# Boundary additions moved to VectorE, transposes per token tile, and narrower first feed-forward pieces in a two-block transformer kernel

## The chip, the cores and the metric

The kernel runs on one NeuronCore of one Trainium2 chip. The metric is the device time of one execution in microseconds (us). Before the change the median of 3 runs is 1402.76 us (1401.82 to 1402.99).

## What is computed

Two transformer blocks run one after the other over 512 tokens of width 1024, in float32. Each block is a mixer (a convolution and attention pair in the first, retention and latent attention in the second), a residual addition, a normalisation, a feed-forward network of hidden width 2816 with a gate and an up half, and a second residual addition. What matters here is the place between two such parts, called a boundary below. Cut to that, the reference says:

```python
x = x + ga1 * rmsnorm(y, post_mix_g)                   # boundary 1, gated
h = rmsnorm(x, pre_ffn_g) * (1.0 + sc2) + sh2
gate, up = jnp.split(h @ w_ffn_in, 2, axis=-1)
x = x + ga2 * rmsnorm(y_ffn, post_ffn_g)               # boundary 2, gated
h = rms_norm(x, attn_norm_w);  proj = h @ w_in_2
x = x + mixed @ w_out                                  # boundary 3, plain
u = rms_norm(x, ffn_norm_w) @ w_up
```

Both norms divide by the root of the mean of squares over the 1024 features of a token.

## The kernel before, in words

The 512 tokens are four token tiles of 128 (tt = 0 to 3), and 1024 features are eight blocks of 128 (kb). Every float32 matrix product is made of three matmuls on split operands (a high part and a low part of each side); `mm3` (lines 201 to 204) issues them, so its three lines carry nearly all the TensorE time.

Weights arrive as slabs of 128x1024. `emit_slab` (lines 175 to 187) loads one into a staging buffer `w_st` (two of them), ScalarE casts it to `w_hi` (line 184), and VectorE, or GpSimd for a few named slabs, subtracts to get `w_lo` (line 207). There are four `w_hi` and four `w_lo` buffers. `slab(key, ahead)` also starts the slabs that follow.

Before each boundary, `gemm_tok` (line 280) makes a product that has tokens on partitions: `wo` before boundary 1, `fout` before boundary 2, `wo2` before boundary 3. The last four slabs stay resident, and the token tiles are finished one after the other, each yielding its PSUM banks, two halves of 512 features. All four `w_hi` buffers are held until the last tile is done.

`boundary` (line 338) takes each token tile as it is yielded. `update` (line 321) adds it to the residual `x`. In the gated case (`grow` given, boundaries 1 and 2) it takes the squares' sums of both halves on ScalarE (`sumsq`, line 247), makes `r` with `rstd` (VectorE line 235, then a power on GpSimd, line 239), multiplies each half on VectorE (line 331) and adds half 0 on VectorE and half 1 on GpSimd (line 334). In the plain case both additions are on VectorE (line 325). Then `norm_of` (line 250) takes one sum of squares over all 1024 features, a second `rstd` (line 233), and writes the normalised tile `xn` (VectorE, line 252).

When `tt` is in `ends`, `to_h` (line 273) transposes the collected `xn` tiles: for each kb, one 128x128 transpose per tile on TensorE (line 228) into a PSUM bank of `psT`, which has two banks, and then `evac_h` (line 254) writes the bank to `hh` and `hl`: ScalarE for `hh` (line 258 or 263), and for `hl` VectorE alone (line 259), or, where there is a bias (boundary 1), VectorE (line 268) and GpSimd (line 207). With `ends=(1, 3)` (boundaries 1 and 3) these are two groups of two tiles, so 256 columns per instruction. With `ends=(1,2,3)` (boundary 2) they are groups of 2, 1 and 1.

After boundaries 1 and 3, `ffn_in` (line 871) starts with four slabs (two pairs of gate and up) and runs them in two column pieces, `t0` = 0 and 256, so that the first half can start before the last tiles are there. In that loop each of the 4 slabs times 8 kb times 3 lines of `mm3` gives 96 matmuls per piece. All later slabs run with 512 columns. After boundary 2 comes a `gemm_tok` on the slabs `c2`, which goes token tile by token tile and has no such pieces.

The order of instructions on each engine is not the program's: the kernel is built in a tile context that schedules over a simulated timeline (line 1448), and the engines' queues then run in that fixed order. `boundary`, `to_h` and `ffn_in` are thus interleaved by the builder.

Of the kernel before, what the change touches and what calls it, by code (L numbers as in the profile page):

```python
# [8 lines left out]
F32 = mybir.dt.float32  # L9
# [4 lines left out]
ALU = mybir.AluOpType  # L14
# [5 lines left out]
KB = 8  # L20
# [75 lines left out]
def build(tc, nc, a):  # L96
    stacks = []

    def pool(name, bufs=1, side="left", **kw):
        s = ExitStack()  # L100
        p = s.enter_context(tc.tile_pool(name=name, bufs=bufs, side=side, reuse_waits="tile", **kw))
        stacks.append(s)
        return p, s

    def close(*ss):
        for s in ss:
            s.close()
# [27 lines left out]
    def pp():  # L135
        Banks.at = (Banks.at + 1) % 6
        if Banks.both and Banks.at % 3 == 0:
            return conv_bank()
        ps_p = psP.tile([128, 512], F32, tag="p", name="ps_p")
        return ps_p  # L140
# [5 lines left out]
    eps1k = const.tile([128, 1], F32)  # L146
# [5 lines left out]
    an32 = const.tile([128, 16], F32)  # L152
# [5 lines left out]
    hh = hpool.tile([128, KB, S], F32R)  # L158
    hl = hpool.tile([128, KB, S], F32R)
# [33 lines left out]
    def slab(key, ahead=2):  # L193
        assert ORDER[W.got] == key, (ORDER[W.got], key)
        W.got += 1
        if W.nxt < W.got:
            emit_slab()
        prefetch(ahead)
        return W.ready.pop(key)

    def mm3(out, lh, ll, rh, rl, start, stop):
        nc.tensor.matmul(out=out, lhsT=lh, rhs=rh, start=start, stop=False)  # L202
        nc.tensor.matmul(out=out, lhsT=lh, rhs=rl, start=False, stop=False)  # L203
        nc.tensor.matmul(out=out, lhsT=ll, rhs=rh, start=False, stop=stop)  # L204
# [11 lines left out]
    def mtile(ps, w, rh, rl, nk, width, c0=0, t0=0, t1=S):  # L216
        wh, wl = w
        for k in range(nk):
            c = k * width + c0
            mm3(  # L220
                ps[:, t0:t1], wh[:, c:c + 128], wl[:, c:c + 128],
                rh[:, k, t0:t1], rl[:, k, t0:t1], k == 0, k == nk - 1,
            )
# [6 lines left out]
    def rstd(ss0, ss1, n_eps):  # L230
        q = sm.tile([128, 1], F32, tag="q", name="q")
        if ss1 is None:
            nc.vector.tensor_tensor(out=q, in0=ss0, in1=n_eps, op=ALU.add)
        else:
            nc.vector.scalar_tensor_tensor(  # L235
                out=q, in0=ss0, scalar=ss1, in1=n_eps, op0=ALU.add, op1=ALU.add
            )
        r = sm.tile([128, 1], F32, tag="r", name="r")
        nc.gpsimd.tensor_tensor(out=r, in0=q, in1=mhalf[:, 0:1], op=ALU.pow)  # L239
        return r  # L240

    def sumsq(src, jp):
        ss = sm.tile([128, 1], F32, tag="ss", name="ss")
        n = src.shape[1]
        w = 256 if n <= 256 else 1024
        junk = jp.tile([128, w], BF16, tag=f"junk{w}", name="junk", bufs=1)
        nc.scalar.activation(out=junk[:, :n], in_=src, func=AF.Square, accum_out=ss)
        return ss

    def norm_of(x_t, jp, xn):  # L250
        r = rstd(sumsq(x_t, jp), None, eps1k)
        nc.vector.tensor_scalar(out=xn, in0=x_t, scalar1=r, scalar2=None, op0=ALU.mult)
# [20 lines left out]
    def to_h(xns, t0, scale, bias, ep):  # L273
        n = len(xns) * 128
        for kb in range(KB):
            ps = pt()
            transposes(ps, [xn[:, kb * 128:(kb + 1) * 128] for xn in xns])
            evac_h(ps[:, :n], kb, t0, n, scale(kb), bias(kb) if bias else None, ep)
# [39 lines left out]
    def h_operand(k):  # L318
        return hh[:, k, :], hl[:, k, :]

    def update(banks, tt, x_in, x_out, grow, bp):
        if grow is None:
            for hf in range(2):
                cs = slice(512 * hf, 512 * hf + 512)
                nc.vector.tensor_tensor(out=x_out[:, cs], in0=banks[tt, hf], in1=x_in[:, cs], op=ALU.add)
            return
        r = rstd(sumsq(banks[tt, 0], bp), sumsq(banks[tt, 1], bp), eps1k)
        for hf in range(2):
            cs = slice(512 * hf, 512 * hf + 512)
            y = bp.tile([128, 512], F32, tag="y", name="y", bufs=2)  # L330
            nc.vector.scalar_tensor_tensor(
                out=y, in0=banks[tt, hf], scalar=r, in1=grow[:, cs], op0=ALU.mult, op1=ALU.mult
            )
            (nc.vector if hf == 0 else nc.gpsimd).tensor_tensor(
                out=x_out[:, cs], in0=x_in[:, cs], in1=y, op=ALU.add
            )

    def boundary(gen, x_in, x_out, grow, scale, bias, bp, after=None, ends=(1, 3)):
        xns = []
        for tt, banks in gen:  # L340
            xi, xo = x_in(tt), x_out(tt)
            update(banks, tt, xi, xo, grow, bp)
            xn = bp.tile([128, D], F32, tag="xn", name="xn", bufs=3)
            norm_of(xo, bp, xn)
            if after:
                after(tt, xo)
            xns.append(xn)
            if tt in ends:
                to_h(xns, 128 * (tt + 1 - len(xns)), scale, bias, bp)
                xns = []  # L350

    class ADA:
        pool, tag, bufs, nacc = ring, "st", NST, 1
# [96 lines left out]
    for _n in ("pre_mix_g", "pre_ffn_g"):  # L450
        _o = VOFF[_n]
        nc.vector.tensor_scalar(
            out=vec[:, _o:_o + 8], in0=vec[:, _o:_o + 8], scalar1=32.0, scalar2=None, op0=ALU.mult
        )
    _o = VOFF["ada_b"]
    for _i in (_o + 8, _o + 32):
        nc.vector.tensor_scalar(
            out=vec[:, _i:_i + 8], in0=vec[:, _i:_i + 8], scalar1=1.0, scalar2=None, op0=ALU.add
# [5 lines left out]
        out=lat[:, 0:2], in0=vec[:, _o:_o + 2], scalar1=float(np.float32(16.0 * 96.0 ** -0.5)), scalar2=None,  # L464
        op0=ALU.mult,
    )
    nc.vector.tensor_scalar(
        out=lat[:, 2:3], in0=vec[:, _o + 2:_o + 3], scalar1=float(np.float32(np.sqrt(128.0))), scalar2=None,
        op0=ALU.mult,
# [135 lines left out]
    gen = gemm_tok([("v", i) for i in range(4)], h_operand, 512, 2, seg=2)  # L605
# [229 lines left out]
    for p in range(4):  # L835
# [26 lines left out]
    bp, bp_s = pool("bp1")  # L862
    gen = gemm_tok([("wo", k) for k in range(8)], lambda k: (mh[:, k, :], ml_[:, k, :]), D, 4)
    x1t = lambda tt: x1[:, tt, :]
    boundary(
        gen, x1t, x1t, grow1, lambda kb: modA[:, 1, kb:kb + 1], lambda kb: modB[:, 1, kb:kb + 1], bp
    )
# [3 lines left out]
    def ffn_in(tag, evac, extra=None, split=None):  # L871
        first = []
        for m in range(2):
            first.append((pp(), slab((tag, m)), pp(), slab((tag, NF + m), 2 - m)))
        for t0 in (0, 256):
            for g, wg, u, wu in first:
                mtile(g, wg, hh, hl, KB, 128, 0, t0, t0 + 256)
                mtile(u, wu, hh, hl, KB, 128, 0, t0, t0 + 256)
        for m, (g, _, u, _) in enumerate(first):
            evac(m, g, u)  # L880
        for m in range(2, NF):
            if extra:
                extra(m)
            if m >= NF - 4:
                split(m - NF + 4)
            g = pp()
            mtile(g, slab((tag, m)), hh, hl, KB, 128)
            u = pp()
            mtile(u, slab((tag, NF + m)), hh, hl, KB, 128)
            evac(m, g, u)  # L890
# [17 lines left out]
    grow2 = gpool.tile([128, D], F32)  # L908
# [47 lines left out]
    def fin_extra(m):  # L956
        if m in (4, 8, 12, 16):
            ga_row(1, grow2, ad2, m // 4 - 1)
        if m == 4:
            rotary()  # L960

    ffn_in("fin", evac1, fin_extra, g1)
    close(ad2_s, f_s)
    bp, bp_s = pool("bp2")
    gen = gemm_tok([("fout", k) for k in range(NF)], g1, D, 4)
    x2d = nc.dram_tensor("x2_spill", [S, D], F32, kind="Internal").ap()

    def spill(tt, xo):
        nc.gpsimd.dma_start(out=x2d[tt * 128:(tt + 1) * 128, :], in_=xo)

    boundary(gen, x1t, x1t, grow2, lambda kb: an32[:, kb:kb + 1], None, bp, after=spill, ends=(1,2,3))
    close(bp_s, g_s, x_s)


# [41 lines left out]
    for tt, banks in gemm_tok([("c2", i) for i in range(4)], h_operand, 416, 4, seg=2):  # L1016
        b = banks[tt, 0]
        for j, (c0, c1) in enumerate(((0, 256), (256, 384))):
            r = rstd(sumsq(b[:, c0:c1], cp), None, epsq[:, j:j + 1])
# [6 lines left out]
    def win2_group(gi):  # L1026
        return gemm_tok([("win2", 4 * gi + i) for i in range(4)], h_operand, 512, 2, seg=2)
# [10 lines left out]
    for kb in range(3):  # L1038
# [5 lines left out]
            out=cTl[:, kb, :], in0=ps, scalar=sc, in1=cTh[:, kb, :].bitcast(F32), op0=ALU.mult, op1=ALU.subtract  # L1044
# [14 lines left out]
    gen = win2_group(2)  # L1059
# [234 lines left out]
    bp, bp_s = pool("bp3")  # L1294
    gen = gemm_tok([("wo2", k) for k in WO2], lambda i: h_operand(WO2[i]), D, 4)
    boundary(gen, x3t, x3t, None, lambda kb: an32[:, 8 + kb:9 + kb], None, bp)
    close(bp_s)

# [29 lines left out]
    bp, bp_s = pool("bp4")  # L1328
    gen = gemm_tok([("down", k) for k in range(NF)], g2, D, 4)
    for tt, banks in gen:  # L1330
        x_t = x3[:, tt, :]
        ot = bp.tile([128, D], F32, tag="ot", name="ot", bufs=2)
        ss = []
        for hf in range(2):
            cs = slice(512 * hf, 512 * hf + 512)
# [3 lines left out]
        r = rstd(ss[0], ss[1], eps1k)  # L1339
        for hf in range(2):  # L1340
            cs = slice(512 * hf, 512 * hf + 512)
# [110 lines left out]
```

## Time and profile before

| | |
|---|---|
| median of 3 runs | 1402.76 us |
| the profiled execution | 1402.35 us, of which the span of the trace is 1400.6 us |
| TensorE (PE) busy | 1348.2 us, 96% of the span |
| VectorE (DVE), ScalarE (ACT), GpSimd (POOL) busy | 55%, 41%, 24% |
| granted TensorE clock, mean | 0.99 of full speed |

In the profile a line such as L202 is a line of the kernel. PE is the matmul row of TensorE, PEld its weight loads, which overlap with matmuls. A matmul's duration in the trace holds its pipeline, so a stream is read by the distance between starts. A releaser after an arrow is what ended an engine's wait. The times of the boundaries in the trace are about 372 to 424 us (first), 749 to 795 us (second) and 1017 to 1054 us (third).

### The profile page before, as it was taken

How to read it: one execution, taken by the hardware profiler on the slowest of the kernel's cores; microseconds unless marked ns; L12 is line 12 of the kernel's file. 1: busy time of each engine (PE TensorE's matmuls, PEld its weight loads, DVE VectorE, ACT ScalarE, POOL GpSimd, SP SyncE). 2: the span in 40 equal slices, each digit the busy share in tenths (PEclk: the TensorE clock that was granted, in tenths of full speed). 3: DMA queues.
4: the chain of work that ended last, by engine and by line, in shares of the span. 5: the costliest groups of instructions: out<-in, count | busy, mean ns of one | idle time of the engine just before them, and what ended most of it. 6: DMA issues, size and time to landing. Idle time of an engine off the chain costs nothing.

```text
span 1400.6 us, 17393 instructions
## 1 busy us (share of the span) xinstructions
PE 1348.2 (96%) x6686; PEld 1119.8 (80%) x6686; DVE 769.5 (55%) x1203; ACT 581.2 (41%) x953; POOL 334.7 (24%) x337
## 2 busy tenths in 40 slices
PE   6998999999979999999999999999999999999997
PEld 4786787888878888888887788887888888888886
DVE  3399968477356434323334665788257555554334
ACT  4357655332244322222323526777246433333323
POOL 2279855411150000000002534567020000000000
PEclk9998999999989999999999999999999999999999
DMA  8422133566224334433322322011323332323231
GB/s 323 154 76 88 35 120 120 166 200 197 99 68 141 126 125 128 135 91 94 102 91 93 121 91 92 30 33 46 111 86 120 99 98 93 103 91 105 91 97 69
DMA packets 44578, 152.18 MB, mean 109 GB/s; under 512 B 4912, under 2 KB 7344, under 8 KB 44496
## 3 DMA queue, kind: packets, MB, share of 16 engines
q1 hardware_dynamic: 43008, 146.03, 32.4%
q0 software_dynamic: 1344, 4.84, 0.9%
q8 instruction: 52, 0.85, 0.2%
q14 instruction: 30, 0.25, 0.1%
q10 hardware_dynamic: 144, 0.21, 0.0%
HBM read 146.86 MB, written 4.19 MB: 108 GB/s over the span
## 4 chain that ended last, share of the span: by engine, by line
PE 84%; DVE 7%; ACT 3%; issue 2%; POOL 2%; DMA 1%; SPq 0%; POOLq 0%; ACTq 0%; DVEq 0%
PE ps_p L202 17%; PE ps_p L204 16%; PE ps_p L203 16%; PE ps_c L203 8%; PE ps_c L204 8%; PE ps_c L202 7%; PE ps_t L202 2%; PE ps_t L204 2%; PE ps_t L203 2%; PE ps_t L228 2%; DVE kp L719 1%; PE ps_t L679 1%; DVE ps_c L523 1%; PE ps_t L385 1%; DVE w_lo L207 1%
## 5 line engine op out<-in xcount | busy, mean ns | idle before, releaser
L184 ACT CAST w_hi<-w_st 128x1024 fp32r<-128x1024 f32 (+2 forms) x217 | 225.1, 1040 | 386.1 <-PE ps_p L203 138.7
L207 DVE TENSOR_TENSOR w_lo<-w_st,w_hi 128x1024 fp32r<-128x1024 f32 (+2 forms) x179 | 222.4, 1244 | 235.5 <-ACT w_hi L184 233.8
L203 PE MATMUL ps_p<-hl,w_hi 128*128 128x512 f32 (+1 forms) x740 | 279.6, 379 | 0.4 <-POOL hl L207 0.4
L204 PE MATMUL ps_p<-hh,w_lo 128*128 128x512 f32 (+1 forms) x740 | 278.0, 377 | 1.4 <-DVE w_lo L207 1.4
L202 PE MATMUL ps_p<-hh,w_hi 128*128 128x512 f32 (+1 forms) x740 | 276.5, 382 | 1.9 <-ACT hh L263 1.2
L239 POOL TENSOR_TENSOR r<-q,mhalf 128x1 f32<-128x1 f32 x36 | 20.9, 583 | 764.5 <-DVE q L235 716.7
L202 PEld LDWEIGHTS ps_p<-hh,w_hi 128*128 128x128 f32 x740 | 139.2, 191 | 29.9 <-ACT hh L263 2.5
L204 PEld LDWEIGHTS ps_p<-hh,w_lo 128*128 128x128 f32 x740 | 140.9, 190 | 27.4 <-DVE w_lo L207 2.5
L203 PEld LDWEIGHTS ps_p<-hl,w_hi 128*128 128x128 f32 x740 | 141.1, 191 | 25.8 <-POOL hl L207 1.6
L202 PE MATMUL ps_c<-hh,w_hi 128*128 128x512 f32 (+1 forms) x354 | 130.0, 367 | 3.9 <-ACT hh L263 3.1
L203 PE MATMUL ps_c<-hl,w_hi 128*128 128x512 f32 (+1 forms) x354 | 130.8, 370 | 0.4 <-POOL hl L207 0.4
L204 PE MATMUL ps_c<-hh,w_lo 128*128 128x512 f32 (+1 forms) x354 | 128.8, 364 | 0.0
L207 POOL TENSOR_TENSOR w_lo<-w_st,w_hi 128x1024 fp32r<-128x1024 f32 (+1 forms) x38 | 93.8, 2474 | 57.2 <-ACT w_hi L184 49.0
L207 DVE TENSOR_TENSOR gl<-gf,gh 128x512 fp32r<-128x512 f32 x44 | 30.4, 690 | 105.6 <-ACT gh L899 105.6
L899 ACT CAST gh<-gf 128x512 fp32r<-128x512 f32 x44 | 27.4, 622 | 133.4 <-PE ps_p L203 124.1
L202 PEld LDWEIGHTS ps_c<-hh,w_hi 128*128 128x128 f32 x354 | 67.6, 191 | 15.3 <-ACT hh L263 3.3
L203 PEld LDWEIGHTS ps_c<-hl,w_hi 128*128 128x128 f32 x354 | 67.2, 190 | 10.9 <-POOL hl L207 0.6
L204 PEld LDWEIGHTS ps_c<-hh,w_lo 128*128 128x128 f32 x354 | 67.5, 191 | 10.2
L204 PE MATMUL ps_p<-w_hi,gl 128*128 128x512 f32 x176 | 68.6, 390 | 0.0
L203 PE MATMUL ps_p<-w_lo,gh 128*128 128x512 f32 x176 | 68.5, 389 | 0.0
L202 PE MATMUL ps_p<-w_hi,gh 128*128 128x512 f32 x176 | 68.5, 389 | 0.0
L523 DVE SCALAR_TENSOR_TENSOR ps_c<-upad,vec,ps_c 128x512 f32<-128x512 f32 x87 | 60.6, 747 | 0.7
(428 smaller groups left out, 2564.3 us busy)
## 6 DMA issues: line engine op xcount, KB each, us to landing
ad<-in_ada SPq DMA_DIRECT2D x48, 512.0 KB, 4.1
w_st<-in_w_fin SPq DMA_DIRECT2D x44, 512.0 KB, 3.7
w_st<-in_w_up SPq DMA_DIRECT2D x44, 512.0 KB, 3.4
w_st<-in_w_win SPq DMA_DIRECT2D x22, 512.0 KB, 3.6
w_st<-in_w_fout SPq DMA_DIRECT2D x22, 512.0 KB, 3.5
w_st<-in_w_down SPq DMA_DIRECT2D x22, 512.0 KB, 3.5
w_st<-in_w_gate SPq DMA_DIRECT2D x16, 512.0 KB, 3.7
w_st<-in_w_wo SPq DMA_DIRECT2D x16, 512.0 KB, 3.8
```

Source lines behind the costliest of these rows:

```text
L184: nc.scalar.copy(w_hi[:, :n], w_st[:, :n])
L202: nc.tensor.matmul(out=out, lhsT=lh, rhs=rh, start=start, stop=False)
L203: nc.tensor.matmul(out=out, lhsT=lh, rhs=rl, start=False, stop=False)
L204: nc.tensor.matmul(out=out, lhsT=ll, rhs=rh, start=False, stop=stop)
L207: (eng or nc.vector).tensor_tensor(out=out, in0=src, in1=hi.bitcast(F32), op=ALU.subtract)
L228: nc.tensor.transpose(out=ps[:r, j * 128:(j + 1) * 128], in_=s, identity=ident)
L239: nc.gpsimd.tensor_tensor(out=r, in0=q, in1=mhalf[:, 0:1], op=ALU.pow)
L385: nc.tensor.matmul(out=ps[32 * b:32 * b + 32, 0:256], lhsT=cact[:, 4 * hf + b, :], rhs=ad[:, b, :], start=hf == 0, stop=hf == 1,)
L523: nc.vector.scalar_tensor_tensor(out=out, in0=src, scalar=w, in1=acc, op0=ALU.mult, op1=ALU.add)
L679: nc.tensor.matmul(out=ps[:, kb * 128:S], lhsT=vt(kb, h), rhs=a_slice(at[j], kb, 0, n), start=first, stop=kb == NT - 1 and j == 0,)
L719: nc.vector.tensor_tensor_scan(out=kp[:, :n][:, ::-1], data0=kp[:, :n][:, ::-1], data1=zero.broadcast_to([128, n]), initial=1.0, op0=ALU.m ...
L899: nc.scalar.copy(gh, gf[:, k, :])
```

## The change

The addition of half 1 in the gated case moves from GpSimd to VectorE. The sum of squares of the new `x` is taken per half, right after each half's addition, instead of once over 1024 features, and `rstd` adds the two. The default `ends` goes from (1, 3) to (0, 1, 3), and boundary 2 from (1, 2, 3) to (0, 1, 2, 3). `ffn_in` runs its first four slabs in pieces of 128, 128 and 256 columns in place of 256 and 256.

```diff
     def update(banks, tt, x_in, x_out, grow, bp):
-        if grow is None:
-            for hf in range(2):
-                cs = slice(512 * hf, 512 * hf + 512)
-                nc.vector.tensor_tensor(out=x_out[:, cs], in0=banks[tt, hf], in1=x_in[:, cs], op=ALU.add)
-            return
-        r = rstd(sumsq(banks[tt, 0], bp), sumsq(banks[tt, 1], bp), eps1k)
+
+        if grow is not None:
+            r = rstd(sumsq(banks[tt, 0], bp), sumsq(banks[tt, 1], bp), eps1k)
+        ss = []
         for hf in range(2):
             cs = slice(512 * hf, 512 * hf + 512)
-            y = bp.tile([128, 512], F32, tag="y", name="y", bufs=2)
-            nc.vector.scalar_tensor_tensor(
-                out=y, in0=banks[tt, hf], scalar=r, in1=grow[:, cs], op0=ALU.mult, op1=ALU.mult
-            )
-            (nc.vector if hf == 0 else nc.gpsimd).tensor_tensor(
-                out=x_out[:, cs], in0=x_in[:, cs], in1=y, op=ALU.add
-            )
-
-    def boundary(gen, x_in, x_out, grow, scale, bias, bp, after=None, ends=(1, 3)):
+            y = banks[tt, hf]
+            if grow is not None:
+                y = bp.tile([128, 512], F32, tag="y", name="y", bufs=2)
+                nc.vector.scalar_tensor_tensor(
+                    out=y, in0=banks[tt, hf], scalar=r, in1=grow[:, cs], op0=ALU.mult, op1=ALU.mult
+                )
+            nc.vector.tensor_tensor(out=x_out[:, cs], in0=y, in1=x_in[:, cs], op=ALU.add)
+            ss.append(sumsq(x_out[:, cs], bp))
+        return ss
+
+    def boundary(gen, x_in, x_out, grow, scale, bias, bp, after=None, ends=(0, 1, 3)):
         xns = []
         for tt, banks in gen:
             xi, xo = x_in(tt), x_out(tt)
-            update(banks, tt, xi, xo, grow, bp)
+            ss = update(banks, tt, xi, xo, grow, bp)
             xn = bp.tile([128, D], F32, tag="xn", name="xn", bufs=3)
-            norm_of(xo, bp, xn)
+            nc.vector.tensor_scalar(out=xn, in0=xo, scalar1=rstd(ss[0], ss[1], eps1k), scalar2=None, op0=ALU.mult)
...
-        for t0 in (0, 256):
+        for t0, t1 in ((0, 128), (128, 256), (256, 512)):
             for g, wg, u, wu in first:
-                mtile(g, wg, hh, hl, KB, 128, 0, t0, t0 + 256)
-                mtile(u, wu, hh, hl, KB, 128, 0, t0, t0 + 256)
+                mtile(g, wg, hh, hl, KB, 128, 0, t0, t1)
+                mtile(u, wu, hh, hl, KB, 128, 0, t0, t1)
...
-    boundary(gen, x1t, x1t, grow2, lambda kb: an32[:, kb:kb + 1], None, bp, after=spill, ends=(1,2,3))
+    boundary(gen, x1t, x1t, grow2, lambda kb: an32[:, kb:kb + 1], None, bp, after=spill, ends=(0, 1, 2, 3))
```

## Rows read from the trace of the kernel before

**Rows 1.** The page's first part: engine, busy us, share of the span, instructions.

```profile
PE 1348.2 (96%) x6686; PEld 1119.8 (80%) x6686; DVE 769.5 (55%) x1203; ACT 581.2 (41%) x953; POOL 334.7 (24%) x337
```

**Rows 2.** Stretches of the three boundaries: length, busy us by engine, clock, DMA share, GB/s.

```profile
core 0: us, PE busy (x) PEld busy (x) DVE busy (x) ACT busy (x) POOL busy (x), PEclk, DMA share, GB/s
...
386.00:393.00 7.00, 0.64 (x3) 0.41 (x4) 4.76 (x8) 3.88 (x9) 2.36 (x3) 0.79 0.58 188
393.00:400.30 7.30, 6.75 (x29) 5.94 (x30) 6.63 (x10) 4.46 (x10) 4.17 (x5) 0.50 0.48 144
400.30:405.00 4.70, 4.31 (x38) 4.07 (x36) 2.92 (x5) 1.87 (x3) 3.17 (x5) 1.00 0.00 0
405.00:424.00 19.00, 18.70 (x156) 18.50 (x156) 6.20 (x13) 6.91 (x14) 8.90 (x12) 1.00 0.00 1
...
764.00:780.00 16.00, 12.85 (x69) 10.36 (x67) 14.22 (x22) 9.99 (x24) 7.75 (x8) 1.00 0.52 175
780.00:795.00 15.00, 13.57 (x67) 10.36 (x68) 12.53 (x46) 9.58 (x30) 8.94 (x12) 1.00 0.19 66
...
1026.00:1034.00 8.00, 6.41 (x49) 5.61 (x47) 5.72 (x10) 5.35 (x11) 3.60 (x2) 1.00 0.44 134
1034.00:1054.00 20.00, 20.00 (x171) 20.00 (x171) 5.93 (x11) 5.14 (x11) 4.11 (x3) 1.00 0.23 79
```

**Rows 3.** Waits of PE, 372 to 430 us: who for whom, total us, times, longest.

```profile
PE ps_t L228 <- DVE xn L252: 3.3, 1, 3.3
PE ps_c L202 <- ACT hh L263: 3.1, 1, 3.1
```

**Rows 4.** ScalarE in order of time, first boundary: start, us, line, operation, idle before.

```profile
383.69 2.00 ACT L184 CAST w_hi<-w_st 128x1024 fp32r<-128x1024 f32 x2 [2.33 <-PE ps_p L204]
...
391.24 1.04 ACT L184 CAST w_hi<-w_st 128x1024 fp32r<-128x1024 f32 x1 [3.05 <-DMA w_st<-in_w_fin]
392.19 1.02 ACT L263 ACTIVATE hh<-ps_t,modB,modA 128x256 fp32r<-128x256 f32 x2
```

**Rows 5.** PE in order of time: 256-column matmuls at the slow clock, then one kb period.

```profile
396.33 0.41 PE L202 MATMUL ps_c<-hh,w_hi 128*128 128x256 f32 x1
396.55 0.41 PE L203 MATMUL ps_p<-hl,w_hi 128*128 128x256 f32 x1
...
411.25 0.38 PE L228 MATMUL ps_t<-identr,xn 128*128 128x128 f32 x2
...
412.90 0.38 PE L228 MATMUL ps_t<-identr,xn 128*128 128x128 f32 x2
```

**Rows 6.** PE in order of time, second block's attention: 128-column matmuls in a row.

```profile
920.60 0.22 PE L202 MATMUL ps_p<-kT,qh 128*128 128x128 f32 x1
920.66 0.27 PE L203 MATMUL ps_p<-kT,qh 128*128 128x128 f32 x1
920.77 0.28 PE L204 MATMUL ps_p<-kT,ql 128*128 128x128 f32 x1
...
922.14 0.28 PE L1224 MATMUL ps_c<-mask,identr 128*128 128x128 f32 x1
922.25 0.27 PE L1224 MATMUL ps_p<-mask,identr 128*128 128x128 f32 x1
```

**Rows 7.** The chain that ended last, a run of transposes: start, us, what.

```profile
852.07 0.87 PE ps_t L228 x8
```

**Rows 8.** The first tile's xn on DVE, and its first transposes on PE.

```profile
380.79 0.75 DVE L252 TENSOR_SCALAR xn<-x,r 128x1024 f32<-128x1024 f32 x1 [0.67 <-POOL r L239]
...
385.31 0.38 PE L228 MATMUL ps_t<-identr,xn 128*128 128x128 f32 x2
```

**Rows 9.** Line 334's instructions: duration in ns, least, median and most.

```profile
L334 DVE TENSOR_TENSOR x<-x,y x8: 678/683/1617, 376.9 to 778.7; 128x512 f32<-128x512 f32 x8
L334 POOL TENSOR_TENSOR x<-x,y x8: 1261/1558/1674, 377.2 to 778.5; 128x512 f32<-128x512 f32 x8
```

**Rows 10.** Line 259's instructions: duration in ns, 128- and 256-column forms.

```profile
L259 DVE SCALAR_TENSOR_TENSOR hl<-ps_t,an,hh x40: 333/472/486, 766.8 to 1051.6; 128x256 fp32r<-128x256 f32 x24, 128x128 fp32r<-128x128 f32 x16
```

## The prediction

> **What bounds the kernel now.** The page's first part comes first: TensorE is busy 96% of the span [rows 1], so a change pays where TensorE idles or is slowed, and it costs wherever it adds TensorE time elsewhere. Next come the stretches of the three boundaries [rows 2], which show how much TensorE loses at each.
>
> At boundary 1 TensorE is busy 0.64 of the 7.00 us from 386 to 393, an idle 6.4 us. From 393 to 400.3 the granted clock is 0.50, that is the lower level of 1.2 GHz, after that idle stretch; it is 1.00 (2.4 GHz) again from 400.3. Of 6.75 busy us there, half, 3.4 us, is the price of the clock. Idle bits of 0.5 and 0.4 us to 405 make 10.7 us that could be got back. From 405 to 424 TensorE is full (18.70 of 19).
>
> The waits name the idle time: 3.3 us for the second tile's xn and 3.1 us for hh [rows 3]. ScalarE's order of time shows the second: the first hh, at 392.19, stands in the queue behind a cast of a weight slab that waited for its DMA until 391.24 [rows 4].
>
> At boundary 2 TensorE is idle 3.2 us from 764 to 780 and 1.4 us from 780 to 795, with VectorE at 14.22 of 16 us: 4.6 us to win, on a nearly full VectorE [rows 2]. At boundary 3 it idles 1.6 us from 1026 to 1034, at full clock, and is full from 1034 to 1054 [rows 2]. **There is hardly anything to win at boundary 3.**
>
> **The narrower pieces.** Each of the two first-slab loops has 96 matmuls per column piece. The first piece of 256 becomes two of 128, so 96 matmuls become 192; the second stays. The old price is in the order of time: a kb period of two transposes and twelve 256-column matmuls lasts 412.90 - 411.25 = 1.65 us [rows 5]. Transposes in a row take 0.87 / 8 = 0.11 us each [rows 7], so a 256-column matmul costs (1.65 - 0.22) / 12 = 0.12 us.
>
> The trace has no such stream of 128-column pieces, so their price is bounded. Where three of them follow one another, the starts are 0.06 and then 0.11 us apart, and two later ones are 0.11 apart [rows 6]; the transposes, also 128 columns and each with its own weight load, are 0.11 apart over eight [rows 7]. The lower bound is 0.06, the upper 0.115. I take 0.11, because every run of more than two shows it: each matmul brings a weight load of 128 columns, and once no wider matmul hides it, the load sets the pace. Halving the columns thus halves next to nothing. The Trainium skill's page TensorE: Matmul & The Clock Gate, section LDWEIGHTS, puts a load of 128 columns at 107 ns, which fits that spacing.
>
> So each loop gains 96 x (0.11 + 0.11 - 0.12) = 9.6 us of TensorE work, and there are two loops. At the slow clock even a 256-column matmul costs 0.22 [rows 5], so none of the new work should be paid there twice.
>
> **Boundary 1.** With ends at 0 the first tile's transposes no longer wait for the second tile's xn. Its xn also comes earlier: the GpSimd addition (1.56 us median) becomes a VectorE one of 0.68 [rows 9], and the squares of half 0 overlap with half 1's addition; about 1 us per tile. It was ready at 381.5, but its transposes stood in TensorE's queue at 385.3, at the end of the product [rows 8], and I expect them about a microsecond earlier, not four.
>
> The casts of the first two slabs end at 385.7 [rows 4], so the first tile's matmuls with them (48 x 0.11 = 5.3 us) can fill most of the gap. They come at the pace of the evacuation: two PSUM banks, each with a transpose, a ScalarE and a VectorE pass, of which the last shrinks from 0.47 to only 0.33 us when the columns are halved [rows 10]. I take 5 of the 6.4 idle us and 2 of the clock's 3.4 as won, 7 in all, and 2.5 to 10.7 as the ends. The net is 9.6 - 7 = **+2.6 us** (-1.1 to +7.1).
>
> What is late next is the slab supply: the third slab is cast only at 391.24 to 392.3, after its DMA [rows 4], which the change does not touch. On VectorE it adds four additions (2.7 us) and eight more evacuations (8 x (2 x 0.33 - 0.47) = 1.5 us); on ScalarE four more squares and eight evacuations. These lie beside TensorE's longer work and I cost them at nothing; if the cover fails, they delay `w_lo`, inside the range above.
>
> **Boundary 2.** No pieces change here. The first tile's transposes can be evacuated before the product ends, and GpSimd's additions go. Against it, VectorE takes four more additions and eight more evacuations, 2.7 + 1.5 = 4.2 us, in a stretch where it is busy 14.22 of 16 us [rows 2]; a part returns, as the longest VectorE addition was 1.62 against 0.68 while GpSimd worked [rows 9]. GpSimd's queue, with the spill DMAs and the powers, gets shorter. The bounds are all idle time won (-4.6) and the VectorE work unhidden less two such stretches (4.2 - 1.9 = +2.3). I take **-2 us**, under half of the idle time, since the last tile's chain through VectorE stays.
>
> **Boundary 3.** The additions were on VectorE already; what is new is the squares per half, the extra group and the pieces. Idle time of 1.6 us can shrink to some 0.6, because `w_lo` of the first slabs is not earlier. Net 9.6 - 1.0 = **+8.6 us**, from 96 x (2 x 0.107 - 0.12) - 1.6 = +7.4 to 96 x (2 x 0.115 - 0.12) = +10.6.
>
> **Sum.** 2.6 - 2 + 8.6 = +9.2 us on the profiled execution's 1402.35, so 1411.6 us. That execution is 0.4 us under the median of the runs, which I neglect. Adding all lower ends gives 1404, all upper ends 1422.
>
> **The rivals.**
>
> *The pieces cost their columns (faster).* If loads hide behind the matmuls of other slabs, as in the 0.06 step [rows 6], 192 x 0.06 equals 96 x 0.12 and nothing is paid. Then 0 - 7, -2 and 0 - 1 make -10: 1392.4 us. For it speaks that one step; against it that no second step in a row shows it. The point that decides is the price at which 2 x 96 x (2p - 0.12) equals the 10 us won: p = 0.086 us. Chance 13%.
>
> *A price between (no change).* If 0.06 and 0.11 alternate, the mean is 0.085, each loop pays 96 x 0.05 = 4.8 us, and the sum is -2.2 - 2 + 3.8 = -0.4: 1401.9 us. For it speaks that the builder may mix wider matmuls in; against it that in the loops all are 128 wide until the first half is done. Chance 14%. The Trainium skill's page TensorE: Matmul & The Clock Gate, section Back-to-back issue gap, gives 81 ns per matmul for a sustained stream at 128 columns; by that figure, as an estimate, the sum would be 1400.4, and the rows' 0.11 contradicts it.
>
> *The tiles come no earlier.* If the builder leaves the new transposes where they stood [rows 8], or ScalarE's queue still puts hh behind a waiting cast [rows 4], the pieces are paid and nothing is won: 9.6 + 0 + 9.6 = +19.2, 1421.6 us. Against it: program order puts the first tile's group before the other tiles. Chance 5%.
>
> **How the numbers follow.** The forecast has 68%. The range must also take in the no-change rival, so it runs from 1400 to 1420; outside stay the faster rival and the extreme of the slow one, together under 20%. A measurement of this kernel can tell about 0.2%, 2.8 us, from no change. Slower gets 0.66 of the forecast, 0.03 of the middle and 0.05 of the last rival, 0.74; the same 0.11; faster 0.15. The slower cases' own range is 1405.6 to 1421.
>
> **What would show it.** In the profile after, the starts of 128-column matmuls in both loops 0.11 us apart, 384 of them; boundary 3 from the end of `wo2` to the first 512-column slab some 8 to 10 us longer; the gap after `wo` under 2 us; no 128-wide matmul at 0.06 for long. I am wrong if those starts stand 0.06 to 0.09 apart, or if the granted clock falls in the loops, which no row here shows at full work.

## The result and the profile after

After the change the median is 1454.45 us (4 runs, 1437.86 to 1458.23), beside 1402.88 us before; the ratio is 1.0344 (95% interval 1.0305 to 1.0384). The kernel is slower by some 52 us, where 9 were forecast: the sign was right, the size was far off. The profiled execution took 1451.85 us, 1449.9 of it the span.

The first part of the page after, and the clock row of its second part (the span in 40 slices, the granted clock of each in tenths):

```profile
PE 1401.9 (97%) x6878; PEld 1172.8 (81%) x6878; DVE 776.3 (54%) x1235; ACT 589.7 (41%) x1001; POOL 323.3 (22%) x337
...
PEclk9998999999859999999999999999969999999999
```

TensorE has 192 matmuls more than in [rows 1], as the diff says, and is busy 53.7 us longer, though no multiplication was added. The clock row shows why: slices 11, 12 and 30 read 8, 5 and 6, where the kernel before has 9, 8 and 9. They hold the two first-slab loops.

To see at which boundary the time was lost, two marks are followed: the first sum of squares of boundary 2 and the load of `x_spill` behind it. Both are from the order of time of ScalarE and GpSimd; here they are before the change:

```profile
749.81 0.60 ACT L247 ACTIVATE junk<-ps_t 128x512 bf16<-128x512 f32 x1 [6.20 <-PE ps_t L204]
...
999.10 0.84 POOL L1292 DMA_DIRECT2D x<-x_spill  x1 [5.59 <-DVE hl L207]
```

And after it:

```profile
771.18 0.60 ACT L247 ACTIVATE junk<-ps_t 128x512 bf16<-128x512 f32 x1 [6.20 <-PE ps_t L204]
...
1023.26 0.84 POOL L1292 DMA_DIRECT2D x<-x_spill  x1 [5.64 <-DVE hl L207]
```

Boundary 1 costs 771.18 - 749.81 = +21.4 us, the part with boundary 2 (1023.26 - 999.10) - 21.4 = +2.8, and the rest, which has boundary 3, what is left of the span's 49.3: +25.1. Forecast were +2.6, -2 and +8.6. The same reading is used for every experiment below.

The stretches of the boundaries after the change, with the columns of [rows 2]; the first four lines have the times of [rows 2]:

```profile
386.00:393.00 7.00, 5.22 (x29) 4.46 (x29) 6.02 (x12) 5.36 (x14) 3.23 (x6) 0.82 0.58 188
393.00:400.30 7.30, 7.26 (x35) 7.07 (x35) 6.61 (x13) 4.63 (x12) 3.26 (x6) 0.50 0.49 144
400.30:405.00 4.70, 4.70 (x25) 4.70 (x25) 3.03 (x7) 2.14 (x6) 0.55 (x1) 0.50 0.00 0
405.00:424.00 19.00, 19.00 (x94) 19.00 (x94) 2.59 (x7) 2.42 (x6) 3.48 (x8) 0.50 0.00 1
...
390.60:433.90 43.30, 43.26 (x207) 43.02 (x207) 16.02 (x31) 12.87 (x30) 10.76 (x21) 0.50 0.12 37
433.90:440.00 6.10, 6.10 (x51) 6.10 (x50) 1.54 (x3) 2.15 (x4) 1.44 (x2) 0.92 0.01 3
...
1050.00:1062.50 12.50, 9.78 (x82) 8.93 (x80) 8.72 (x14) 6.49 (x15) 6.03 (x4) 1.00 0.41 132
1062.50:1093.00 30.50, 30.50 (x151) 30.50 (x150) 3.90 (x10) 4.10 (x11) 1.04 (x1) 0.51 0.09 33
1093.00:1104.00 11.00, 11.00 (x92) 11.00 (x91) 2.42 (x5) 2.75 (x6) 0.00 (x0) 0.97 0.00 0
```

The idle time of boundary 1 is indeed filled: 5.22 of 7 us are busy, where it was 0.64. But from 390.6 to 433.9 us TensorE is busy 43.26 of 43.30 us at a granted clock of 0.50, that is 1.2 GHz. At boundary 3 the same lasts 30.5 us. Before, the slow stretch was 7.3 us long at boundary 1, and there was none at boundary 3 [rows 2]. Half of 43.3 and of 30.5 us, 36.9 us, is the price of the clock in the changed kernel.

The order of time of TensorE at the fall, at about 390.5 us, and at the return, before 435 us (start, us, what):

```profile
389.11 0.28 PE L204 MATMUL ps_c<-hh,w_lo 128*128 128x128 f32 x1
389.22 0.27 PE L202 MATMUL ps_c<-hh,w_hi 128*128 128x128 f32 x1
389.33 0.28 PE L203 MATMUL ps_p<-hl,w_hi 128*128 128x128 f32 x1
...
391.36 0.41 PE L202 MATMUL ps_c<-hh,w_hi 128*128 128x128 f32 x1
391.58 0.41 PE L203 MATMUL ps_p<-hl,w_hi 128*128 128x128 f32 x1
391.79 0.41 PE L204 MATMUL ps_p<-hh,w_lo 128*128 128x128 f32 x1
...
431.89 0.41 PE L204 MATMUL ps_c<-hh,w_lo 128*128 128x128 f32 x1
432.10 0.52 PE L202 MATMUL ps_c<-hh,w_hi 128*128 128x256 f32 x1
...
435.36 0.28 PE L204 MATMUL ps_c<-hh,w_lo 128*128 128x256 f32 x1
435.48 0.28 PE L202 MATMUL ps_c<-hh,w_hi 128*128 128x256 f32 x1
```

At full clock the narrow matmuls start 0.11 us apart, as forecast. At the lower level they start 0.21 to 0.22 apart, no less than 256-column ones did there [rows 5]. The whole narrow stream ran to its end at the lower level; the first 256-column matmul starts at 432.10, and by 435.36 these start 0.12 us apart, at full clock again.

The scatter of the runs points the same way: 1437.86 us had a mean clock of 0.978, 1451.85 had 0.967, 1457.06 had 0.962 and 1458.23 had 0.960.

### The profile page after: what moved, and what is told of

It reads as the page before. It is cut to its first block, busy times and chain, and to the rows that moved or that the text cites. A ratio compares the mean times of both kernels' runs of the same rounds, so it can differ in the third digit from the quotient of the medians.

```text
span 1449.9 us, 17904 instructions
## 1 busy us (share of the span) xinstructions
PE 1401.9 (97%) x6878; PEld 1172.8 (81%) x6878; DVE 776.3 (54%) x1235; ACT 589.7 (41%) x1001; POOL 323.3 (22%) x337
## 4 chain that ended last, share of the span: by engine, by line
PE 87%; DVE 6%; ACT 3%; issue 2%; DMA 1%; POOL 1%; SPq 0%; POOLq 0%; ACTq 0%; DVEq 0%
PE ps_p L202 17%; PE ps_p L203 17%; PE ps_p L204 17%; PE ps_c L204 8%; PE ps_c L202 8%; PE ps_c L203 8%; PE ps_t L228 2%; PE ps_t L202 2%; PE ps_t L204 2%; PE ps_t L203 2%; DVE kp L719 1%; PE ps_t L679 1%; DVE ps_c L523 1%; PE ps_t L385 1%; ACT w_hi L184 1%
## 5 line engine op out<-in xcount | busy, mean ns | idle before, releaser
L203 PE MATMUL ps_p<-hl,w_hi 128*128 128x512 f32 (+2 forms) x772 | 295.6, 383 | 0.4 <-POOL hl L207 0.4
L204 PE MATMUL ps_p<-hh,w_lo 128*128 128x512 f32 (+2 forms) x772 | 293.6, 381 | 1.0 <-DVE w_lo L207 1.0
L202 PE MATMUL ps_p<-hh,w_hi 128*128 128x512 f32 (+2 forms) x772 | 291.7, 385 | 1.5 <-ACT hh L263 1.2
L239 POOL TENSOR_TENSOR r<-q,mhalf 128x1 f32<-128x1 f32 x36 | 21.4, 596 | 802.7 <-DVE q L235 781.6
L202 PEld LDWEIGHTS ps_p<-hh,w_hi 128*128 128x128 f32 x772 | 152.1, 200 | 29.5 <-ACT hh L263 2.5
L202 PE MATMUL ps_c<-hh,w_hi 128*128 128x512 f32 (+2 forms) x386 | 145.2, 378 | 2.1 <-ACT hh L263 1.4
L203 PE MATMUL ps_c<-hl,w_hi 128*128 128x512 f32 (+2 forms) x386 | 146.2, 379 | 0.1
L204 PE MATMUL ps_c<-hh,w_lo 128*128 128x512 f32 (+2 forms) x386 | 145.0, 376 | 0.0
L202 PEld LDWEIGHTS ps_c<-hh,w_hi 128*128 128x128 f32 x386 | 80.8, 210 | 13.6 <-ACT hh L263 1.8
L203 PEld LDWEIGHTS ps_c<-hl,w_hi 128*128 128x128 f32 x386 | 81.5, 211 | 10.6 <-POOL hl L207 0.3
L204 PEld LDWEIGHTS ps_c<-hh,w_lo 128*128 128x128 f32 x386 | 81.3, 211 | 10.2
```

## The experiments

Ten further kernels, told by what they tell apart. The shifts are those of the profiled execution against the kernel before, in us, at the marks above.

| kernel | median us | ratio (95%) | boundary 1 | 2 | 3 |
|---|---|---|---|---|---|
| the change | 1454.45 | 1.0344 (1.0305 to 1.0384) | +21.4 | +2.8 | +25.1 |
| boundary parts only | 1415.37 | 1.0087 (1.0074 to 1.0101) | +3.2 | +2.8 | +7.8 |
| pieces only | 1460.61 | 1.0412 (1.0398 to 1.0427) | +29.0 | +1.6 | +29.2 |
| pieces only, wide one first | 1421.13 | 1.0129 (1.0115 to 1.0143) | +9.2 | +0.8 | +8.6 |
| the change, pieces 128 and 384 | 1423.51 | 1.0163 (1.0136 to 1.0190) | +9.6 | +1.5 | +9.2 |
| the change, columns doubled | 1422.08 | 1.0136 (1.0121 to 1.0151) | +4.1 | +2.1 | +12.5 |
| additions and squares only | 1402.59 | 1.0000 (0.9991 to 1.0009) | -0.3 | +1.4 | 0.0 |
| additional groups only | 1418.39 | 1.0113 (1.0096 to 1.0130) | +3.0 | +3.6 | +9.4 |
| first pair alone, doubled | 1402.45 | 1.0003 (0.9994 to 1.0012) | +1.6 | -0.3 | -0.3 |
| first pair alone, narrow | 1404.17 | 1.0014 (1.0005 to 1.0023) | +1.7 | -0.1 | -0.1 |
| idle time filled by hand | 1403.17 | 1.0002 (0.9993 to 1.0011) | -0.5 | +2.7 | +0.1 |

**Is it the pieces or the boundary?** The changed kernel with its old pieces:

```diff
-        for t0, t1 in ((0, 128), (128, 256), (256, 512)):
+        for t0, t1 in ((0, 256), (256, 512)):
```

> The change without its narrower pieces: additions on VectorE, squares per half, transposes per token tile stay; the first four slabs run in pieces of 256 and 256 again. Theory A (the 128-column pieces are the loss: the weight loads set their pace at 0.11 us and the granted clock falls to 0.50 while they run): 1398 to 1405 us, granted clock 0.98 to 0.99. Rival B (the per-tile transposes, evacuations and VectorE additions are the loss, the pieces only run while TensorE waits anyway): 1425 us or more.

It came to 1415.37 us, between the two ranges. So most of the loss needs the pieces, but the boundary parts by themselves cost 12 us, where 7 + 2 + 1 = 10 us of gain had been counted on. Where that comes from is followed up further down. The other half, the pieces in the kernel before:

```diff
-        for t0 in (0, 256):
+        for t0, t1 in ((0, 128), (128, 256), (256, 512)):
```

> The kernel before with nothing changed but the pieces, 128, 128 and 256. Theory A: nearly the whole loss, 1440 to 1460 us, granted clock 0.96 to 0.97, with the clock at 0.50 through most of both loops. Rival B: 1420 us or less.

1460.61 us, just above the first range: the pieces alone cost 58 us, more than the whole change, and at boundary 3 with no other edit there. Its stretches, columns as above:

```profile
393.00:440.00 47.00, 46.14 (x219) 45.54 (x219) 16.11 (x27) 12.19 (x24) 15.65 (x20) 0.50 0.08 23
...
1062.00:1066.00 4.00, 2.77 (x20) 2.27 (x18) 1.61 (x2) 2.08 (x4) 0.72 (x1) 1.00 0.49 157
1066.00:1106.00 40.00, 40.00 (x191) 39.89 (x191) 5.86 (x13) 4.57 (x10) 3.35 (x3) 0.50 0.08 29
1106.00:1112.00 6.00, 6.00 (x48) 6.00 (x47) 3.28 (x4) 3.45 (x4) 0.00 (x0) 0.90 0.18 62
```

Both loops run slow until a few us into their 256-column piece. Behind an idle 1.2 us at 1062 to 1066 the clock falls and stays down for 40 us of unbroken work.

**Load price or clock?** The same narrow matmuls, as many, but behind the wide piece:

```diff
-        for t0 in (0, 256):
+        for t0, t1 in ((0, 256), (256, 384), (384, 512)):
```

> The kernel before with pieces of 256, 128 and 128 (the narrow ones last, when no tile is waited for and TensorE has just been full at 256 columns). Theory A (the narrow stream by itself lets the clock fall): clock 0.50 in the second half of both loops, 1430 to 1460 us. Rival G (the clock falls only because of the idle stretch between the product and the first slabs, and then merely lasts): at the third boundary, where the wide pieces start at full clock, it stays 1.00, each loop pays only the 9.6 us of the weight loads, 1418 to 1426 us.

1421.13 us, as the rival of the clock that merely lasts had it. The stretches of the first loop and of the third boundary's:

```profile
393.00:402.00 9.00, 7.82 (x36) 7.12 (x37) 7.25 (x11) 5.47 (x12) 5.14 (x7) 0.53 0.35 120
402.00:412.00 10.00, 9.82 (x83) 9.59 (x83) 5.62 (x11) 4.32 (x8) 6.21 (x7) 1.00 0.01 2
412.00:434.00 22.00, 22.00 (x201) 22.00 (x200) 7.72 (x11) 9.31 (x13) 5.09 (x7) 1.00 0.15 44
...
1046.00:1070.00 24.00, 24.00 (x216) 24.00 (x215) 7.57 (x13) 6.47 (x12) 2.84 (x3) 1.00 0.13 45
```

Here the wide piece brings the clock back by 402 us as before, and the narrow stream that follows keeps it at 1.00 for 22 us. What is left is +9.2 and +8.6 us per loop, beside the 9.6 of the forecast's sum: that price was right, and it is only this price. So a narrow stream that follows wide work at full clock without a break did not pull the clock down; in the kernels that start with it, the clock is not regained until the wide piece.

A narrow piece and then a piece of 384 columns, in the changed kernel:

```diff
-        for t0, t1 in ((0, 128), (128, 256), (256, 512)):
+        for t0, t1 in ((0, 128), (128, 512)):
```

> The change with pieces of 128 and 384 columns in place of 128, 128 and 256: half as many narrow matmuls, 96 per loop, and no more matmuls than before the change. Theory A: the clock falls in the 128 piece and comes back in the 384 one, so some 10 us of slow clock and 4 us of weight loads per loop against what the change wins: 1412 to 1435 us. If the weight loads alone cost (clock near 0.99): 1402 to 1410 us.

1423.51 us, 31 us less than the change (one of its four executions took 1433.19 us, at a mean clock of 0.974 beside 0.983 and 0.984). In two stretches of its first loop the granted clock tells when it comes back:

```profile
394.00:414.00 20.00, 18.25 (x85) 16.97 (x84) 11.29 (x24) 8.84 (x25) 7.29 (x15) 0.50 0.18 52
...
418.00:420.00 2.00, 2.00 (x14) 2.00 (x13) 0.00 (x0) 0.00 (x0) 0.89 (x2) 1.00 0.00 0
```

It is 1.00 again by 418 us, when the wide piece is under way, some 17 us sooner than in the change.

**Does the width hold the clock, or the waits?** All the above also shift when tiles are needed. So the order, the number of matmuls and their waits were kept, and only their width changed: the first piece runs the first tile's columns twice side by side, the second piece runs columns 0 to 255 again.

```diff
+    def twice(ps, w):
+        wh, wl = w
+        two = lambda r, k: r[:, k:k + 1, 0:128].broadcast_to([128, 2, 128])
+        for k in range(KB):
+            c = k * 128
+            mm3(
+                ps[:, 0:256].rearrange("p (a b) -> p a b", a=2), wh[:, c:c + 128], wl[:, c:c + 128],
+                two(hh, k), two(hl, k), k == 0, k == KB - 1,
+            )
...
-                mtile(g, wg, hh, hl, KB, 128, 0, t0, t1)
-                mtile(u, wu, hh, hl, KB, 128, 0, t0, t1)
+                for ps, w in ((g, wg), (u, wu)):
+                    if t0 == 0:
+                        twice(ps, w)
+                    else:
+                        mtile(ps, w, hh, hl, KB, 128, 0, t0 if t0 == 256 else 0, t1)
```

> The changed kernel, in which each narrow matmul of the first two pieces is made 256 columns wide without another instruction: the first piece runs the first tile's 128 columns twice side by side, the second runs columns 0 to 255 again from the start, the third is as it was. Work is added; the number of matmuls, their order and their waits stay. Theory (the clock stays at its lower level because the stream is narrow): the granted clock comes back within about 10 us in both loops, as it does in the kernel before, each of the 384 matmuls costs 0.12 us against 0.11, that is +4 us, and the 37 us of half speed nearly go: 1415 to 1428 us, mean clock 0.985 or more. So the kernel with more work is faster than the changed one by 27 to 40 us. Rival (the idle bits and waits around the tiles pull the clock down and keep it there, the width does not matter): slow stretches of some 43 and 31 us as in the changed kernel, mean clock 0.965 to 0.97, 1450 to 1462 us.

1422.08 us: with twice the columns in 384 matmuls the kernel is 32 us **faster** than the change. Its stretches:

```profile
386.00:388.50 2.50, 1.34 (x5) 0.77 (x6) 2.48 (x5) 2.47 (x9) 1.22 (x3) 1.00 0.48 91
388.50:393.50 5.00, 5.00 (x28) 4.72 (x27) 4.37 (x8) 3.38 (x6) 2.02 (x4) 0.66 0.57 219
393.50:428.00 34.50, 34.23 (x287) 33.99 (x286) 15.87 (x32) 14.01 (x32) 15.01 (x23) 1.00 0.11 31
...
1032.00:1044.00 12.00, 10.29 (x80) 9.34 (x79) 8.34 (x14) 6.39 (x14) 6.05 (x4) 1.00 0.43 136
1044.00:1072.00 28.00, 28.00 (x238) 28.00 (x238) 6.33 (x15) 6.50 (x16) 1.04 (x1) 1.00 0.10 37
```

The clock falls in boundary 1 just as in the change, and is back at 1.00 from 393.5 us on; at boundary 3 it never falls, with 1.7 us of idle time from 1032 to 1044. The rival is out for how long the clock stays low: in the change it stayed at 0.50 through 43.3 us with hardly a wait in them, and with twice the columns it was back by 393.5 us. For the fall itself at boundary 3 the two kernels differ in idle time too, 2.7 us of 12.5 in the change and 1.7 of 12 here, so there the width is not told from the idle time.

**Where do the boundary parts lose 12 us?** The kernel before with the additions and squares alone (the new `update`, old `ends` and pieces), and with the additional groups alone (the old `update`); the second one's edit:

```diff
-    def boundary(gen, x_in, x_out, grow, scale, bias, bp, after=None, ends=(1, 3)):
+    def boundary(gen, x_in, x_out, grow, scale, bias, bp, after=None, ends=(0, 1, 3)):
...
-    boundary(..., after=spill, ends=(1,2,3))
+    boundary(..., after=spill, ends=(0, 1, 2, 3))
```

> The kernel before with one part of the change: additions on VectorE and sums of squares per half; the transposes keep their groups of two (and 2, 1, 1) and the first slabs their two pieces of 256. Theory (the 12 us of the boundary parts without the pieces come from the additional group of transposes, which stands alone in TensorE's queue since the first matmuls still need the second tile): 1399 to 1405 us, the third boundary within 1 us of before. Rival (four more VectorE additions and the doubled squares on ScalarE are what delays the boundaries): 1410 to 1417 us, and the third boundary some 7 us later than before.

> The kernel before with the other part alone: one group of transposes more at each boundary (first tile by itself), additions and squares as before, pieces of 256. Theory (the additional group is the cost): 1410 to 1418 us, TensorE idle for 6 to 9 us at the third boundary with waits of transposes for hl, the granted clock at 0.50 behind that. Rival (the additions and squares are the cost): 1401 to 1406 us, the third boundary within 1 us of before.

1402.59 and 1418.39 us, the second just above its range. By themselves the additions and squares are worth nothing and cost nothing; the additional groups cost it all. The longest waits of TensorE at the third boundary, and two of its stretches, in the kernel with the groups alone:

```profile
PE ps_t L228 <- DVE hl L259: 6.8, 4, 2.7
...
1032.00:1040.00 8.00, 2.58 (x11) 1.34 (x9) 5.35 (x11) 4.52 (x10) 3.57 (x2) 0.68 0.41 131
1040.00:1046.00 6.00, 4.40 (x19) 3.74 (x19) 2.32 (x6) 2.56 (x6) 2.89 (x2) 0.50 0.53 154
```

With pieces of 256 columns no matmul can start on the first tile alone. Its transposes stand at the head of TensorE's queue and go at the pace of two PSUM banks and their evacuation, 6.8 us of waits for `hl`, and nothing lies beside them; the clock falls to 0.50 behind that. With both edits (boundary parts only) the loss is 3 us smaller than with the groups alone.

**A version from the findings.** The additions and squares of the change, the additional group only at boundary 1, and there the first tile's columns alone only for the first pair of slabs, once doubled by `twice` and once narrow:

```diff
-        for t0, t1 in ((0, 128), (128, 256), (256, 512)):
+        if tag == "up":
+            steps = ((0, 0, 256), (1, 0, 256), (0, 256, 512), (1, 256, 512))
+        else:
+            steps = ((0, 0, 128), (1, 0, 256), (0, 128, 512), (1, 256, 512))
+        for pair, t0, t1 in steps:
...
```

> A version made from the findings. The additions and squares are those of the change. The additional group of transposes is left only at the first boundary; the other two have their groups of before, and the second block's first slabs their two pieces of 256. In the first block the first pair of slabs runs the first tile's 128 columns alone, doubled to 256 columns, then the second pair runs columns 0 to 255, the first pair 128 to 511, the second pair 256 to 511. Theory (columns hold the clock, and the first tile's matmuls fill the idle time): about 7 us of the 10.7 us of idle time and half speed at the first boundary are won; the first pair pays 48 x (0.12 + 0.17 - 0.24) = 2.4 us; 1394 to 1400 us, the clock back at 1.00 before 395 us. Rival (the supply of tiles and casts sets the end of the loop, not TensorE): 1400 to 1405 us, as before.

> The same, but the first pair runs the first tile's 128 columns once, in 48 narrow matmuls. Theory (narrow matmuls don't bring the clock back): the granted clock stays at 0.50 until those 48 are through, some 10 us after 389 us in place of some 4, so this is 2 to 4 us slower than the doubled version, 1397 to 1403 us, though it has half the columns there. Rival (48 narrow matmuls are too few to matter): the same time as the doubled version within 1 us, or less.

1402.45 and 1404.17 us; neither beats the kernel before. The same 13 us in both, the doubled one first:

```profile
390.00:403.00 13.00, 10.65 (x67) 9.26 (x65) 11.69 (x23) 8.09 (x19) 6.39 (x13) 0.87 0.48 156
```

```profile
390.00:403.00 13.00, 11.47 (x54) 10.60 (x52) 11.53 (x21) 8.29 (x20) 6.31 (x11) 0.51 0.39 135
```

The mean clock is 0.87 with doubled columns and 0.51 with narrow ones, as the theory says. But in these two executions the loop ends at the same time (shifts +1.6 and +1.7), and the doubled one idles more instead, 2.4 us of the 13 beside 1.5: part of what it gains in clock it waits for tiles. The doubled version's time is the one that the rival of its expectation gave, that the supply sets the end. Between the two versions the executions shown can't decide: they lie 0.4 us apart, while the medians of 11 runs each differ by 1.7 us, with the narrow one slower. That is between the two expectations (2 to 4 us, and within 1), so the clock may be worth something here too, but far less than in the change.

**The idle time filled by hand.** The kernel before, with wide matmuls on operands already there, behind the product before boundary 1:

```diff
+    g0 = pp()
+    for i in range(16):
+        nc.tensor.matmul(out=g0, lhsT=identr, rhs=mh[:, i % 8, :], start=i == 0, stop=i == 15)
...
```

> The kernel before, and nothing of the change, with 16 more matmuls of 512 columns on operands that are already there, in a bank that the first gate slab starts over afterwards. They stand in TensorE's queue right behind the product before the first boundary, so they fill 16 x 0.23 = 3.6 us of its idle time, up to the second tile's xn. Their results are not used. Theory (the idle stretch, not the narrow transposes, is what lets the clock fall at the first boundary, and wide work holds it): the granted clock stays at 1.00 through 393 to 400 us, or falls for under 3 us, and the 3.4 us of half speed come back in part: 1398.5 to 1401 us. Rival (the idle time that is left before hh, some 3 us, is enough, or the tiles' supply sets the end anyway): the same time as before, 1402 to 1404 us.

1403.17 us (ratio 1.0002, 0.9993 to 1.0011): no change. Its stretches show the fall only put off:

```profile
385.00:389.20 4.20, 4.20 (x21) 3.38 (x20) 3.31 (x5) 2.77 (x7) 0.84 (x3) 1.00 0.44 124
389.20:395.20 6.00, 2.29 (x11) 1.38 (x9) 5.57 (x7) 4.17 (x7) 3.39 (x4) 0.79 0.61 216
395.20:399.50 4.30, 4.30 (x22) 4.25 (x21) 3.94 (x6) 2.15 (x6) 3.12 (x4) 0.50 0.45 128
```

From 389.2 us on TensorE idles 3.7 us of 6, and the clock falls behind that instead.

## Why the prediction was wrong

**The price of the narrow matmuls was right.** The term of 9.6 us per loop measured 9.2 and 8.6 with the narrow stream at 1.00 (wide piece first), and the starts are 0.11 us apart. The two rivals with lower prices are out.

**The idle time of boundary 1 was won, as counted.** Of 7.6 idle us from 386 to 424 [rows 2] 1.8 are left, 5.8 won where the sum had 5. The gap behind `wo` was forecast at under 2 us; TensorE's longest wait for `hh` there is 1.4 us:

```profile
PE ps_c L202 <- ACT hh L263: 1.4, 1, 1.4
```

**The step that failed** is the clause on the clock: "none of the new work should be paid there twice". The sum prices every narrow matmul at 0.11 us. At boundary 1 some 179 of the 192 ran at the lower level, at 0.21 to 0.22, and at boundary 3 some 119. The forecast counted 2 of the 3.4 us of the slow stretch as won, which takes it that narrow work after the gap brings the clock back as the 256-column matmuls had done [rows 2]. With 128-column matmuls in their place it lasted 43.3 us. So boundary 1 is 9.6 for the pieces, less 5.8 for the idle time, plus (43.3 - 7.3) / 2 = 18.0 for the clock: +21.8, beside 21.4 measured. Boundary 3 is 9.6 + 30.5 / 2 = 24.9, beside 25.1. The clock is thus 33 us above the kernel before, and with the 2 us counted as won 35 of the 40 us that the forecast missed; the other 5 are boundary 2's. Two smaller misses cancel: boundary 1 won 5.8 us of idle time where 5 were counted, and boundary 3 did not win its 1 (2.7 us are idle from 1050 to 1062.5). The forecast named the fall of the clock as what would make it wrong ("if the granted clock falls in the loops"), but no rival carried it and the range left it out. [rows 5] held a hint at the price, not at how long it would be paid: at the lower level a 256-column matmul costs 0.22, twice its price, and the 0.11 of a narrow one could be expected to double as well.

**Boundary 2** was forecast at -2 and came to +2.8. The kernel with the groups alone has +3.6 there and the one with additions alone +1.4; but the pieces alone and the idle time filled by hand, with no edit there, have +1.6 and +2.7. Differences of this size at this boundary are thus not resolved by one execution, and the gain of 2 us that was expected from earlier transposes and from GpSimd's shorter queue shows in none of them.

**The additional groups** were costed at nothing, beside TensorE's longer work. In the change that cover is there: it is 6 us faster than the pieces alone. Without the pieces it is gone, and the groups cost 16 us.

Not settled is what lets the clock fall at boundary 3 in the first place. It did after idle bits and narrow work (2.7 us of 12.5 idle in the change, 1.2 of 4 in the pieces alone), and did not after idle bits and wide work (1.7 of 12 with columns doubled, 1.6 of 8 in [rows 2]); a kernel that changes the idle time alone in front of a narrow stream was not tried.

## What to carry over

Cutting a matmul piece from 256 to 128 columns to start earlier saves no TensorE time where each matmul has its own weight load (0.11 us against 0.12), and where it follows an idle bit it can leave the whole stream at half clock until wider matmuls come. Before narrowing, look at what the granted clock is where the piece starts, price the piece at that level to its end, and put wide work first or keep the width. An earlier group of transposes can pay only if there are matmuls that can use its tile alone; otherwise it stands in front of the work and its evacuation is the pace (16 us here). Even with such matmuls the two versions tried at boundary 1 won nothing over the kernel before (1402.45 and 1404.17 us).

## What the hardware showed that was not expected

- TensorE stayed at 0.50 for 43.3 us while busy 43.26 of them, all but the last 1.8 us with 128-column matmuls and transposes, and for 40 us in the kernel with the pieces alone; the same stream held 1.00 for 22 us when it came behind wide matmuls at 1.00.
- More work was faster: doubling the columns of 384 matmuls took the time from 1454.45 to 1422.08 us.
- At 0.50 matmuls of 128 and of 256 columns both start 0.21 to 0.22 us apart; at 1.00 it is 0.11 and 0.12.
